# Mixture-of-experts kernel: down products two chunks behind gate and up, chains cut one group apart, tokens scaled once by 1/rms, and the gather's modulation on ACT

## The chip, the cores and the metric

One Trainium2 chip, one of its cores. The metric is the device time of one execution in microseconds, as a median over runs. The profiled execution is one more run, with its own time and its own span.

## The reference, cut to what matters

The model has two layers on 256 latent tokens of width 1024. Layer 0 is attention, a short convolution and a dense SwiGLU; layer 1 is a spatial gating unit and then eight SwiGLU experts, of which every token uses the best two. All of it is fp32. The change concerns the experts, for which the tokens are first normalised by their rms and modulated (a scale and a shift for each feature):

```python
def modulate(x, g, shift, scale):
    return rmsnorm(x, g) * (1 + scale) + shift

def moe_swiglu(h, router_w, wg, wu, wd):
    logits = (h @ router_w).astype(jnp.float32)
    top_v, top_i = lax.top_k(logits, TOP_K)              # 2 of 8
    gates = jax.nn.softmax(top_v, axis=-1)
    dense_gate = ...                                      # 0 where not chosen
    out = jnp.zeros_like(h)
    for e in range(N_EXPERTS):                            # 8, each 3584 wide
        out = out + dense_gate[..., e:e + 1] * swiglu(h, wg[e], wu[e], wd[e])
    return out
...
    hf = modulate(h, norm_ffn_g[i], sf, cf)
    h = h + gf * moe_swiglu(hf, router_w[j], moe_w_gate[j], moe_w_up[j], moe_w_down[j])
```

## The kernel before

**Experts, chunks, groups, tiles.** The expert stage streams all weights of all eight experts through the core. An expert's 3584 hidden features are cut into seven chunks of 512. A chunk takes six weight tiles of 1 MB (128 partitions by 2048 fp32): two for gate, two for up, two for down. Two tiles are one *group*, and the program is a list of groups, made in the same order in `Weights.__init__` (for the loads) and in the loop at the end (for the work): gate of chunk ci, up of chunk ci, down of chunk ci−1. So the down product of an expert's last chunk comes behind gate and up of the next expert's chunk 0.

**Splits.** TensorE works on fp32 values that are split into a high and a low part. For each tile `Weights.split` issues an ACT cast of the raw tile `mw` to its high part `mh` and a DVE subtraction that gives the low part `ml`. There are six raw buffers, five for high parts and five for low parts. SP issues the next load when the split of an old tile has released its buffer. `group` issues the splits of the tiles a few ahead, and behind the second of three it runs what is in the list `late`.

**Light and heavy experts.** The tokens of an expert are gathered by a one-hot matrix product into at most 128 rows. With at most 64 tokens ("light") the token operand holds high and low part side by side, and each k-slice takes two matmuls of 512 columns (`products`, lines 1078 and 1079); otherwise ("heavy") it takes three (`mm3`, lines 142 to 144). Which of the two a group runs is decided on TensorE by a branch on a count in memory.

**The chain of a chunk.** TensorE makes the gate and up rows (`m_0_0`, `m_0_1`), ACT copies them to SBUF (line 1138), TensorE turns them (line 1146), ACT makes the silu of gate (`m_sg`, line 1152), DVE multiplies with up (line 1153), ACT and DVE split the result into high and low part, `moe_aT` (lines 217 and 218), and the down product reads that (`m_y`). `moe_aT` has two buffers.

**The chain of an expert.** *Gather*, in the preceding expert: DVE makes six one-hot tiles (lines 1098 and 1101), of which `ohs` carries the factor 1/rms of each token; TensorE multiplies `h` by it (line 1109); the result is modulated by `m_m.a` and `m_m.b` out of PSUM, four instructions on DVE for the first half of the features (line 1118) and four on ACT for the second (line 1116), and split to `m_xg`. *Scatter*, in the following expert: behind the last down product DVE scales `m_y` (line 1173, `m_yg`), ACT and DVE split it (`m_yhi`, `m_ylo`), and four scatter products `m_sc` (line 1182) are each added to `moe_acc` by a DVE instruction (line 1184). For expert 0 that instruction reads `h` in place of `moe_acc`.

**What sets the order.** Every engine executes in program order, and that order is decided when the program is built: by the lists `late` and `todo_after` of the loop, and by a scheduler behind them. A DVE instruction that waits for TensorE holds every split that stands behind it.

Of the kernel before, what the change touches and what calls it, by code (L numbers as in the profile page):

```python
# [18 lines left out]
P = 128  # L19
D = 1024  # L20
KT = D // P
S = 256
# [52 lines left out]
def hybrid_kernel(  # L75
# [185 lines left out]

    def ada_rows(pa, name, w=512):
        rw = xp.tile([P, 512], F32, tag="rw", name=name + "_rw", bufs=2)
        A.copy(rw[:, :w], pa[:, :w])
        flush()
        return rw
# [59 lines left out]
    def ada_v(layer, n, half):  # L326

        r = ada_load(layer, n, half)
        if half == 0:
            held[0] = xp.tile([P, 512], F32, tag="rw", name=f"adv{layer}_{n}", bufs=2)  # L330
# [576 lines left out]

    class Weights:
# [86 lines left out]
    h = slot(2, "h")[:, :NT * D].rearrange("p (t d) -> p t d", t=NT)  # L995
    for t in range(NT):
        for b in range(2):
# [3 lines left out]
            copied = A.copy(h[:, t, b * 512:(b + 1) * 512], pt)  # L1001
# [45 lines left out]
    acc = slot(4, "moe_acc")[:, :NT * D].rearrange("p (t d) -> p t d", t=NT)  # L1047
# [38 lines left out]
    class Expert:  # L1086


        def __init__(self, e, pos, xg_slot, n):
            self.e, self.n, self.pos = e, n, pos  # L1090
            self.xg = in_pairs(slot(xg_slot, n + "_xg", F32R)[:, :2 * KT * P], KT)

        def positions(self):
            oh2 = x2k(self.n + "_oh")
            self.oh, self.ohs = oh2[:, :S], oh2[:, S:]
            self.ohd = x2k(self.n + "_ohd")[:, :S]
            for t in range(NT):
                V.tensor_scalar(self.ohs[:, t * P:(t + 1) * P], iota, one(self.pos, t, self.e), rstd[t], op0=ALU.is_equal, op1=ALU.mult)
# [4 lines left out]
        def gather(self, b, pool=None):  # L1103
            n = self.n
            pg = bank(f"{n}_pg{b}", pool or psd)
            for i in range(4):
                k = 4 * b + i
                for t in range(NT):
                    T.matmul(pg[:, i * P:(i + 1) * P], h[:, t, k * P:(k + 1) * P], self.ohs[:, t * P:(t + 1) * P],
                             start=(t == 0), stop=(t == NT - 1))  # L1110
# [39 lines left out]
        def act(self, ci, pts):  # L1150
# [3 lines left out]
            self.aT = in_pairs(at[:, 1024 * (ci % 2):1024 * (ci % 2) + 1024], 4)  # L1154
            split_pairs(self.aT, sg)

        def down(self, ci, parts, light):
            aT = self.aT
# [7 lines left out]
        def down_half(self, i, parts, light):  # L1166

            for k in range(4):
                products(self.y[i], self.aT, k, tuple(w[:, k, :] for w in parts[0]), light, False, k == 3)

        def gated(self, i):
            src = x2k(f"{self.n}_yg{i}")
            V.tensor_tensor(src, self.y[i], gf1[:, i * 512:(i + 1) * 512], op=ALU.mult)
            y = [x2k(f"{self.n}_y{x}{i}", F32R) for x in ("hi", "lo")]
# [3 lines left out]
        def scatter(self, t, i, y, first=False, pool=None):  # L1178
# [4 lines left out]
            av, was = (a[:, t, i * 512:(i + 1) * 512] for a in (acc, h if first else acc))  # L1183
            V.scalar_tensor_tensor(av, ps, one(gate, t, self.e), was, op0=ALU.mult, op1=ALU.add)
# [16 lines left out]
    for b in range(2):  # L1201
        ex.gather(b, psb)
    behind["V"] = ex.made.ins
    W.load(8)
    lights = [None] * NE
    step, todo_after = 0, {}

    def after(n, f):
        todo_after.setdefault(step + n, []).append(f)

    late = []

    def group(light, body, then=lambda: None):
# [11 lines left out]
        late.append(then)  # L1225
# [161 lines left out]
```

## Time and profile before

| | |
|---|---|
| median of 3 runs (lowest to highest) | 1474.3 us (1472.17 to 1477.77) |
| profiled execution: device time, span | 1478.5 us, 1476.7 us |
| PE busy in the span | 1390.9 us (94%) |
| DVE busy | 1226.8 us (83%) |
| ACT busy | 974.0 us (66%) |
| the expert stage, from the first `m_ohT` to the end | 968.8 us |

PE is TensorE, PEld its weight loads, DVE is VectorE, ACT is ScalarE. An expert's begin is taken here as the moment at which ACT writes its `m_ohT`: 507.87, 629.92, 745.22, 861.17, 977.15, 1106.34, 1237.31 and 1352.98 us. The experts 0, 4 and 5 run heavy, the other five light. A busy share is an average over stages with different limits; the rows further down are taken from single stages.

### The profile page before, as it was taken

Reading aid. Unit: us, or ns where it says so; the run is one execution under the profiler, and the core shown is the slowest. Engines: PE = TensorE matmul, PEld = TensorE weight load, DVE = VectorE, ACT = ScalarE, POOL = GpSimd, SP = SyncE. Lnnn points to the kernel's source line nnn. Section 1 sums busy time; section 2 is a strip of 40 time slices with the busy share of each in tenths; the row PEclk is TensorE's granted clock in tenths of the full one; section 3 lists DMA queues with packets and bytes.
Section 4 is the critical chain, followed back from the end, with each engine's and each line's share of the span. In section 5 each row is a group of like instructions: output and inputs, shape, how many; then the busy total and the mean of one; then the engine's idle time right before and its main releaser. Section 6 shows DMA issues by size and latency. Waiting matters only on the chain.

```text
span 1476.7 us, 19854 instructions
## 1 busy us (share of the span) xinstructions
PE 1390.9 (94%) x7746; PEld 1151.7 (78%) x7746; DVE 1226.8 (83%) x1256; ACT 974.0 (66%) x891; POOL 1.9 (0%) x7
## 2 busy tenths in 40 slices
PE   6999999999999999999989989999999999899897
PEld 4667789999979888877767767777888888677675
DVE  4687588776666698899999998998888879899897
ACT  3444354433354576788887887886777768788785
POOL 0000000000000000000000000000000000000000
PEclk9999999999999999999999999999999999999999
DMA  9554488776654698899998998998978988899894
GB/s 367 226 219 166 155 335 323 286 274 251 245 224 176 240 402 330 326 340 395 403 398 343 408 398 334 416 385 338 365 294 331 365 343 349 331 421 386 336 413 189
DMA packets 66784, 473.53 MB, mean 321 GB/s; under 512 B 7376, under 2 KB 7760, under 8 KB 9696
## 3 DMA queue, kind: packets, MB, share of 16 engines
q1 hardware_dynamic: 66464, 471.16, 82.0%
q8 instruction: 93, 1.52, 0.4%
q0 software_dynamic: 192, 0.56, 0.2%
q14 instruction: 35, 0.29, 0.1%
HBM read 470.64 MB, written 1.05 MB: 319 GB/s over the span
## 4 chain that ended last, share of the span: by engine, by line
PE 59%; DVE 20%; issue 9%; ACT 8%; DMA 5%; DVEq 0%; SPq 0%; ACTq 0%
DVE ml L949 13%; ACT mh L948 5%; PE m L142 5%; PE m L144 5%; PE m L143 5%; PE fg_ps L164 4%; PE fd L164 4%; PE fu_ps L164 4%; PE m_y L144 2%; PE m_y L142 2%; PE m_y L143 2%; PE so_ps L164 2%; PE ada L259 2%; PE su_ps L164 2%; DMA mw<-in_moe_w_gate_dram 1%
## 5 line engine op out<-in xcount | busy, mean ns | idle before, releaser
L949 DVE TENSOR_TENSOR ml<-mw,mh 128x2048 fp32r<-128x2048 f32 x336 | 757.1, 2286 | 47.9 <-ACT mh L948 44.9
L948 ACT CAST mh<-mw 128x2048 fp32r<-128x2048 f32 x336 | 631.2, 1910 | 12.4 <-PE so_ps L164 4.1
L1079 PE MATMUL m<-ml,m_xg 128*128 128x512 f32 x560 | 223.3, 399 | 5.7 <-DVE ml L949 5.7
L1078 PE MATMUL m<-mh,m_xg 128*128 128x512 f32 x560 | 224.1, 400 | 0.0
L1078 PE MATMUL m_y<-mh,moe_aT 128*128 128x512 f32 x280 | 118.2, 422 | 25.3 <-DVE moe_aT L218 21.4
L142 PE MATMUL m<-mh,m_xg 128*128 128x512 f32 x336 | 134.5, 401 | 0.6 <-ACT m_xg L217 0.6
L1079 PE MATMUL m_y<-ml,moe_aT 128*128 128x512 f32 x280 | 121.3, 433 | 13.8 <-DVE ml L949 11.9
L1079 PEld LDWEIGHTS m<-ml,m_xg 128*128 128x128 f32 x560 | 105.2, 188 | 37.0 <-DVE ml L949 14.6
L144 PE MATMUL m<-mh,m_xg 128*128 128x512 f32 x336 | 132.9, 396 | 0.0
L143 PE MATMUL m<-ml,m_xg 128*128 128x512 f32 x336 | 132.7, 395 | 0.0
L1078 PEld LDWEIGHTS m<-mh,m_xg 128*128 128x128 f32 x560 | 105.3, 188 | 22.6
L1079 PEld LDWEIGHTS m_y<-ml,moe_aT 128*128 128x128 f32 x280 | 56.4, 201 | 45.3 <-DVE ml L949 34.3
L1078 PEld LDWEIGHTS m_y<-mh,moe_aT 128*128 128x128 f32 x280 | 56.7, 203 | 41.3 <-ACT mh L948 19.3
L217 ACT CAST moe_aT<-m_sg 128x512 fp32r<-128x512 f32 x56 | 37.4, 669 | 72.5 <-DVE m_sg L1153 72.5
L142 PEld LDWEIGHTS m<-mh,m_xg 128*128 128x128 f32 x336 | 65.6, 195 | 13.3 <-ACT m_xg L217 1.5
L144 PEld LDWEIGHTS m<-mh,m_xg 128*128 128x128 f32 x336 | 65.5, 195 | 12.5
L143 PEld LDWEIGHTS m<-ml,m_xg 128*128 128x128 f32 x336 | 65.7, 196 | 11.9
L1152 ACT ACTIVATE m_sg<-m_t 128x512 f32<-128x512 f32 x56 | 33.6, 599 | 53.5 <-PE m L142 26.7
L144 PE MATMUL m_y<-mh,moe_aT 128*128 128x512 f32 x168 | 66.4, 396 | 0.7 <-DVE moe_aT L218 0.7
L143 PE MATMUL m_y<-ml,moe_aT 128*128 128x512 f32 x168 | 66.4, 395 | 0.0
L142 PE MATMUL m_y<-mh,moe_aT 128*128 128x512 f32 x168 | 66.2, 396 | 0.0
L164 PE MATMUL fd<-a,fd_hi 128*128 128x256 f32 x352 | 63.0, 281 | 0.0
(410 smaller groups left out, 2663.8 us busy)
## 6 DMA issues: line engine op xcount, KB each, us to landing
mw<-in_moe_w_gate_dram SPq DMA_DIRECT2D x112, 1024.0 KB, 7.1
mw<-in_moe_w_up_dram SPq DMA_DIRECT2D x112, 1024.0 KB, 7.1
mw<-in_moe_w_down_dram SPq DMA_DIRECT2D x110, 1024.0 KB, 6.8
ada<-in_ada_w_dram SPq DMA_DIRECT2D x40, 1024.0 KB, 4.9
fg_w<-in_ffn_w_gate_dram SPq DMA_DIRECT2D x11, 1024.0 KB, 5.2
fu_w<-in_ffn_w_up_dram SPq DMA_DIRECT2D x11, 1024.0 KB, 5.4
fd<-in_ffn_w_down_dram SPq DMA_DIRECT2D x11, 1024.0 KB, 5.0
adap<-in_ada_pairs_dram SPq DMA_DIRECT2D x8, 1024.0 KB, 9.6
```

Of the source, the lines that this page charges most:

```text
L142: T.matmul(o, lh, rh, start=start, stop=False)
L143: T.matmul(o, lh, rl, start=False, stop=False)
L144: T.matmul(o, ll, rh, start=False, stop=stop)
L164: self.newest = m = T.matmul(o, lhsT, rhs, start=self.first is None, stop=stop, skip_group_check=True)
L217: A.copy(hi, src)
L259: queued(T.matmul(pa[32 * j:32 * j + 32, :r.shape[2]], stat[:, 4 * half + j, :], r[:, j, :], start=(first and half == 0), stop=(last and h ...
L948: queued(A.copy(hi, r), "A")
L949: queued(V.tensor_tensor(lo, r, hi.bitcast(F32), op=ALU.subtract), "V")
L1078: T.matmul(o, x, wh, start=start, stop=False)
L1079: T.matmul(o, x, wl, start=False, stop=stop)
L1152: A.activation(sg, pts[0], AF.Silu)
```

## The change

It does five things.

1. The down product of a chunk stands two chunks behind its gate and up (`LAG`), in the order of loads and of work; `moe_aT` gets a third buffer. At the program's end one whole down group, that of chunk 5, stands ahead of the two half groups of chunk 6.
2. One list `todo` takes the place of `late` and `todo_after`: the split of `moe_aT`, of `m_yg` and of a gathered half is put a group behind the instructions that make its input.
3. `h` is written as token times 1/rms, out of PSUM by ACT, and a second ACT copy of the same PSUM tile starts `moe_acc` with the unscaled token. So the one-hot tiles need no factor (`ohs` and its two DVE instructions for each expert are gone), and the first addition of a scatter reads `moe_acc` like the others.
4. All eight modulations of a gather are on ACT.
5. The two row buffers `rw` of an earlier stage become halves of one tile, and the third `moe_aT` buffer takes that place later.

```diff
+    LAG = 2
...
-                    if ci:
-                        self.add(self.down(e, ci - 1))
-                    elif e:
-                        self.add(self.down(e - 1, NCH - 1))
+                    if e or ci >= LAG:
+                        self.add(self.down(*divmod(e * NCH + ci - LAG, NCH)))
+            for ci in range(NCH - LAG, NCH - 1):
+                self.add(self.down(NE - 1, ci))
...
-            copied = A.copy(h[:, t, b * 512:(b + 1) * 512], pt)
+            at_ = slice(b * 512, (b + 1) * 512)
+            A.copy(acc[:, t, at_], pt)
+            copied = A.activation(h[:, t, at_], pt, AF.Copy, scale=rstd[t])
...
-            for t in range(NT):
-                V.tensor_scalar(self.ohs[:, t * P:(t + 1) * P], iota, one(self.pos, t, self.e), rstd[t], op0=ALU.is_equal, op1=ALU.mult)
...
-                if b:
-                    A.activation(t32[:, o], pg[:, o], AF.Identity, bias=m_m.b(k), scale=m_m.a[:, k:k + 1])
-                else:
-                    V.tensor_scalar(t32[:, o], pg[:, o], m_m.a[:, k:k + 1], m_m.b(k), op0=ALU.mult, op1=ALU.add)
-            self.made = split_pairs(self.xg[:, 4 * b:4 * b + 4], t32)
+                A.activation(t32[:, o], pg[:, o], AF.Identity, bias=m_m.b(k), scale=m_m.a[:, k:k + 1])
+            self.part[b] = t32
+
+        def cut(self, b):
+            self.made = split_pairs(self.xg[:, 4 * b:4 * b + 4], self.part.pop(b))
...
-            self.aT = in_pairs(at[:, 1024 * (ci % 2):1024 * (ci % 2) + 1024], 4)
-            split_pairs(self.aT, sg)
+
+            def cut():
+                self.aT[ci] = in_pairs(at[((self.e * NCH if isinstance(self.e, int) else 0) + ci) % 3], 4)
+                split_pairs(self.aT[ci], sg)
+
+            return cut
...
-            if n == tiles.stop + 2:
-                while late:
-                    late.pop(0)()
+                for f in todo.pop(step, ()):
+                    f()
...
+    def put_back(x):
+
+        def gate_out():
+            src = [x.gated(i) for i in range(2)]
+
+            def cut():
+                ys = [x.gated_parts(i, src[i]) for i in range(2)]
+                for i in range(2):
+                    for t in range(NT):
+                        then(1 + 2 * i + t, lambda t=t, i=i: x.scatter(t, i, ys[i]))
+
+            then(1, cut)
+
+        then(0, gate_out)
+
+    def gathered(x, b):
+        x.gather(b)
+        then(1, lambda: x.cut(b))
...
+    for ci in range(NCH - LAG, NCH - 1):
+        group(lights[-1], lambda parts, arm: ex.down(ci, parts, arm))
```

The order is shown at three places. The first is DVE where expert 2 takes over from expert 1; `m1_` and `m2_` are the two experts, `ml92` is the low part of weight tile 92, `m2_0_sg` belongs to chunk 0 of expert 2. Before:

```order
L1184 SCALAR_TENSOR_TENSOR moe_acc_4885<-m1_sc00_7633,gate_4792,moe_acc_4885 128x512
L949 TENSOR_TENSOR ml92_7500<-mw92_7318,mh92_7499 128x2048
L1153 TENSOR_TENSOR m2_0_sg_7569<-m2_0_t1_7479,m2_0_sg_7569 128x512
L949 TENSOR_TENSOR ml93_7564<-mw93_7370,mh93_7563 128x2048
L218 TENSOR_TENSOR moe_aT_4884<-m2_0_sg_7569,moe_aT_4884 128x512
L1184 SCALAR_TENSOR_TENSOR moe_acc_4885<-m1_sc10_7693,gate_4792,moe_acc_4885 128x512
...
L949 TENSOR_TENSOR ml94_7577<-mw94_7380,mh94_7576 128x2048
L1184 SCALAR_TENSOR_TENSOR moe_acc_4885<-m1_sc01_7774,gate_4792,moe_acc_4885 128x512
L949 TENSOR_TENSOR ml95_7626<-mw95_7427,mh95_7625 128x2048
```

In the changed kernel the same engine has there:

```order
L1163 TENSOR_TENSOR m2_0_sg_7484<-m2_0_t1_7406,m2_0_sg_7484 128x512
L957 TENSOR_TENSOR ml89_7409<-mw89_7234,mh89_7408 128x2048
L218 TENSOR_TENSOR moe_aT3_4874<-m2_0_sg_7484,moe_aT3_4874 128x512
...
L1201 SCALAR_TENSOR_TENSOR moe_acc_4827<-m1_sc00_7744,gate_4777,moe_acc_4827 128x512
L957 TENSOR_TENSOR ml96_7607<-mw96_7418,mh96_7606 128x2048
L1163 TENSOR_TENSOR m2_1_sg_7684<-m2_1_t1_7594,m2_1_sg_7684 128x512
L957 TENSOR_TENSOR ml97_7671<-mw97_7482,mh97_7670 128x2048
L218 TENSOR_TENSOR moe_aT_4873<-m2_1_sg_7684,moe_aT_4873 128x512
...
L1201 SCALAR_TENSOR_TENSOR moe_acc_4827<-m1_sc10_7808,gate_4777,moe_acc_4827 128x512
L957 TENSOR_TENSOR ml98_7690<-mw98_7493,mh98_7689 128x2048
L1201 SCALAR_TENSOR_TENSOR moe_acc_4827<-m1_sc01_7882,gate_4777,moe_acc_4827 128x512
```

The low part of chunk 0's `moe_aT` has moved from behind tile 93 to behind tile 89, and what stands beside the scatter is now the chain of chunk 1. Between tile 89 and the first addition stand tiles 90 to 95, the two `m_yg` and the two `m_ylo`.

The second place is TensorE at the same point, around the down product of expert 2's chunk 0 (the light branch). Before:

```order
L1182 MATMUL m1_sc10_7693<-m1_yhi0_7489,m1_ohT_5985 128x512
L1182 MATMUL m1_sc10_7693<-m1_ylo0_7490,m1_ohT_5985 128x512
...
L1078 MATMUL m2_y0_7623<-mh92_7499,moe_aT_4884 128x512
...
L1079 MATMUL m2_y1_7624<-ml93_7564,moe_aT_4884 128x512
...
L1182 MATMUL m1_sc01_7774<-m1_yhi1_7495,m1_ohT_5985 128x512
L1182 MATMUL m1_sc01_7774<-m1_ylo1_7496,m1_ohT_5985 128x512
```

Now:

```order
L1199 MATMUL m1_sc10_7808<-m1_yhi0_7676,m1_ohT_5932 128x512
L1199 MATMUL m1_sc10_7808<-m1_ylo0_7677,m1_ohT_5932 128x512
...
L1089 MATMUL m2_y0_7736<-mh96_7606,moe_aT3_4874 128x512
...
L1090 MATMUL m2_y1_7737<-ml97_7671,moe_aT3_4874 128x512
...
L1199 MATMUL m1_sc01_7882<-m1_yhi1_7680,m1_ohT_5932 128x512
L1199 MATMUL m1_sc01_7882<-m1_ylo1_7681,m1_ohT_5932 128x512
```

TensorE's own order at the scatter is the same as before: second scatter, down product of the new expert's chunk 0, third scatter. What moved is the pair of tiles that this down product reads, from 92 and 93 to 96 and 97, against `moe_aT` that is ready earlier.

The third place is ACT where the expert stage begins (`mo` is the PSUM tile with the tokens, `mo_v` is 1/rms, `mh2` and `mh3` are weight splits, `m0_` is expert 0). Before:

```order
L1001 COPY h_4842<-mo01_4849 128x512
L1001 COPY h_4842<-mo10_4855 128x512
L1031 ACT_TABLE_LOAD
L1031 ACTIVATE ex0_5127<-lg_4867,mx0_5124 128x8
...
L1001 COPY h_4842<-mo11_4861 128x512
L948 CAST mh2_4946<-mw2_4932 128x2048
L948 CAST mh3_4952<-mw3_4934 128x2048
...
L217 CAST m0_xg_4891<-m0_t0_4909 128x512
```

Now:

```order
L1011 ACTIVATE h_4826<-mo00_4828,mo_v_4808 128x512
L1011 ACTIVATE h_4826<-mo01_4835,mo_v_4808 128x512
...
L1010 COPY moe_acc_4827<-mo10_4842 128x512
L1011 ACTIVATE h_4826<-mo10_4842,mo_v_4808 128x512
L1010 COPY moe_acc_4827<-mo11_4849 128x512
L1011 ACTIVATE h_4826<-mo11_4849,mo_v_4808 128x512
L956 CAST mh2_4932<-mw2_4918 128x2048
L956 CAST mh3_4938<-mw3_4920 128x2048
L1125 ACTIVATE m0_t0_4895<-m0_pg0_4886,modT_103,a_m_4050 128x128
...
L217 CAST m0_xg_4880<-m0_t0_4895 128x512
```

Ahead of the casts of tiles 2 and 3 there are now eight PSUM reads in place of four, two of them behind a wait for 1/rms; behind the casts stand the first half's four modulations, which were on DVE, ahead of the first `m0_xg`.

## Rows read from the trace of the kernel before

**Rows 1.** The profile's page: busy time of the engines, and the costliest group.

```profile
PE 1390.9 (94%) x7746; PEld 1151.7 (78%) x7746; DVE 1226.8 (83%) x1256; ACT 974.0 (66%) x891; POOL 1.9 (0%) x7
...
L949 DVE TENSOR_TENSOR ml<-mw,mh 128x2048 fp32r<-128x2048 f32 x336 | 757.1, 2286 | 47.9 <-ACT mh L948 44.9
```

**Rows 2.** Windows by expert (0, 1, 2, 7): length, busy times, TensorE clock, DMA share, GB/s.

```profile
507.87:629.92 122.05, 121.80 (x571) 102.87 (x571) 104.14 (x70) 90.20 (x75) 0.00 (x0) 1.00 0.91 348
629.92:745.22 115.30, 106.25 (x514) 83.88 (x513) 111.20 (x78) 97.55 (x82) 0.00 (x0) 1.00 0.97 380
745.22:861.17 115.95, 104.46 (x492) 81.50 (x491) 110.17 (x77) 95.04 (x80) 0.00 (x0) 0.97 0.96 382
1352.98:1476.70 123.72, 103.59 (x466) 78.96 (x464) 109.69 (x72) 90.23 (x74) 0.00 (x0) 0.95 0.81 324
```

**Rows 3.** DVE's waits, experts 2 and 3 (745.22 to 977.15 us): us in total, times, longest.

```profile
DVE moe_acc L1184 <- PE m_sc L1182: 8.9, 2, 4.5
DVE ml L949 <- ACT mh L948: 2.7, 4, 1.2
```

**Rows 4.** The same for the light experts 6 and 7 (1237.31 to 1460 us).

```profile
DVE moe_acc L1184 <- PE m_sc L1182: 8.5, 2, 4.3
```

**Rows 5.** Timeline of DVE as expert 2 takes over: start, duration, [idle before <-releaser].

```profile
768.80 0.69 DVE L218 TENSOR_TENSOR moe_aT<-m_sg,moe_aT 128x512 fp32r<-128x512 f32 x1
...
776.78 0.75 DVE L1184 SCALAR_TENSOR_TENSOR moe_acc<-m_sc,gate,moe_acc 128x512 f32<-128x512 f32 x1 [4.43 <-PE m_sc L1182]
```

**Rows 6.** Timeline of TensorE at the same place.

```profile
769.64 0.76 PE L1078 MATMUL m_y<-mh,moe_aT 128*128 128x512 f32 x1 [4.59 <-DVE moe_aT L218]
...
776.12 0.40 PE L1182 MATMUL m_sc<-m_yhi,m_ohT 128*128 128x512 f32 x1
776.35 0.39 PE L1182 MATMUL m_sc<-m_ylo,m_ohT 128*128 128x512 f32 x1
```

**Rows 7.** Windows, columns as in Rows 2: behind that wait, and a stretch of light chunks.

```profile
772.00:776.00 4.00, 4.00 (x12) 3.13 (x11) 0.35 (x1) 3.05 (x2) 0.00 (x0) 0.56 0.96 358
1400.00:1450.00 50.00, 47.76 (x231) 37.50 (x230) 50.00 (x29) 44.34 (x36) 0.00 (x0) 1.00 1.01 410
```

**Rows 8.** Timeline of DVE: one one-hot tile with its factor, and a gather's modulations.

```profile
703.52 0.34 DVE L1098 TENSOR_SCALAR m_oh<-cst,posm,mo_v 128x128 f32<-128x128 f32 x1
...
717.02 0.40 DVE L1118 TENSOR_SCALAR m_t<-m_pg,a_m,modT 128x128 f32<-128x128 f32 x1
...
719.55 1.04 DVE L1118 TENSOR_SCALAR m_t<-m_pg,a_m,modT 128x128 f32<-128x128 f32 x3
```

**Rows 9.** Timeline of ACT: the other half's modulations.

```profile
723.40 1.50 ACT L1116 ACTIVATE m_t<-m_pg,modT,a_m 128x128 f32<-128x128 f32 x4 [0.33 <-PE m_pg L1109]
```

**Rows 10.** Timeline of ACT where the expert stage begins.

```profile
494.49 1.07 ACT L1001 COPY h<-mo 128x512 f32<-128x512 f32 x2 [0.16 <-PE mo L1000]
...
499.87 0.58 ACT L1001 COPY h<-mo 128x512 f32<-128x512 f32 x1
500.35 3.70 ACT L948 CAST mh<-mw 128x2048 fp32r<-128x2048 f32 x2
```

**Rows 11.** Timeline of TensorE at the same place: the first gather and the first expert matmul.

```profile
501.20 3.73 PE L1109 MATMUL m_pg<-m_oh,h 128*128 128x128 f32 x32
...
506.65 0.51 PE L142 MATMUL m<-mh,m_xg 128*128 128x512 f32 x1 [0.64 <-ACT m_xg L217]
```

**Rows 12.** Timeline of DVE at the end of the program.

```profile
1455.92 4.49 DVE L949 TENSOR_TENSOR ml<-mw,mh 128x2048 fp32r<-128x2048 f32 x2
1460.33 0.69 DVE L1153 TENSOR_TENSOR m_sg<-m_t,m_sg 128x512 f32<-128x512 f32 x1
1461.72 0.69 DVE L218 TENSOR_TENSOR moe_aT<-m_sg,moe_aT 128x512 fp32r<-128x512 f32 x1 [0.71 <-ACT moe_aT L217]
1464.70 0.69 DVE L1173 TENSOR_TENSOR m_yg<-m_y,gf 128x512 f32<-128x512 f32 x1 [2.28 <-PE m_y L1079]
```

**Rows 13.** The page's DMA issues: KB each, us to landing.

```profile
mw<-in_moe_w_gate_dram SPq DMA_DIRECT2D x112, 1024.0 KB, 7.1
```

More of the change, by code (lines that the diff above doesn't have):

```diff
@@ L329, in ada_v @@
         if half == 0:
-            held[0] = xp.tile([P, 512], F32, tag="rw", name=f"adv{layer}_{n}", bufs=2)
+            held[0] = next_rows()
         ac = held[0]
@@ L994, in hybrid_kernel @@
     rstd = st.rstd()
-    h = slot(2, "h")[:, :NT * D].rearrange("p (t d) -> p t d", t=NT)
+    h, acc = (slot(i, n)[:, :NT * D].rearrange("p (t d) -> p t d", t=NT) for i, n in ((2, "h"), (4, "moe_acc")))
     for t in range(NT):
@@ L1046, in hybrid_kernel @@
     at = slot(3, "moe_aT", F32R)
-    acc = slot(4, "moe_acc")[:, :NT * D].rearrange("p (t d) -> p t d", t=NT)
+    at3 = xp.tile([P, 1024], F32R, tag="rw", name="moe_aT3", bufs=1)
+    at = [at[:, :1024], at[:, 1024:2048], at3]
     iota = cst[:, C_IOTA:C_IOTA + P]
@@ L1176, in gated, with scatter @@
             return y
-        def scatter(self, t, i, y, first=False, pool=None):
+        def scatter(self, t, i, y, pool=None):
             ps = bank(f"{self.n}_sc{t}{i}", pool or psd)
@@ L1182, in scatter @@
                 T.matmul(ps, self.ohT[:, t * P:(t + 1) * P], y[o], start=(o == 0), stop=(o == 1))
[L1183 to L1184 removed]
+            av = acc[:, t, i * 512:(i + 1) * 512]
+            V.scalar_tensor_tensor(av, ps, one(gate, t, self.e), av, op0=ALU.mult, op1=ALU.add)
     def store(t, i):
@@ L1202, in hybrid_kernel @@
         ex.gather(b, psb)
+        ex.cut(b)
     behind["V"] = ex.made.ins
@@ L1205, in hybrid_kernel, with then, group @@
     lights = [None] * NE
[L1206 to L1213, printed above, removed]
+    step, todo = 0, {}
+    def then(n, f):
+        todo.setdefault(step + n, []).append(f)
+    def group(light, body):
         nonlocal step
@@ L1230, in turned, with acted @@
         pts = [bank(f"{x.n}_{ci}_t{m}", psb) for m in range(2)]
-        return pts, (lambda arm: x.turn(pts, gu, arm)), (lambda: x.act(ci, pts))
-    nothing = (None, lambda arm: None, lambda: None)
-    prev = None
+        def acted():
+            cut = x.act(ci, pts)
+            then(1, cut)
+        return (lambda arm: x.turn(pts, gu, arm)), acted
+    def put_back(x):
[6 more added lines that the diff above has]
+                        then(1 + 2 * i + t, lambda t=t, i=i: x.scatter(t, i, ys[i]))
+            then(1, cut)
+        then(0, gate_out)
+    def gathered(x, b):
+        x.gather(b)
+        then(1, lambda: x.cut(b))
+    experts = {0: ex}
     for e in range(NE):
-        light = lights[e]
+        light, ex = lights[e], experts[e]
         for ci in range(NCH):
+            turn = None
+            if ci:
+                turn, acted = turned(ex, ci - 1, gu)
+                behind.clear()
             gu = []
-            _, turn, acted = turned(ex, ci - 1, prev[2]) if ci else nothing
-            if ci:
-                behind.clear()
             o = bank(f"{ex.n}_{ci}_0")
@@ L1264, in hybrid_kernel @@
                 flush()
-            if prev is not None:
-                px, pi, _ = prev
+            if e or ci >= LAG:
+                pe, pi = divmod(e * NCH + ci - LAG, NCH)
+                px, turn = experts[pe], None
                 if pi == 0:
@@ L1269, in hybrid_kernel @@
                 if ci == NCH - 1:
[L1270 to L1272 removed]
+                    turn, acted = turned(ex, ci, gu)
                 def downs(parts, arm):
                     px.down(pi, parts, arm)
[L1276 to L1286 removed]
+                    if turn:
+                        turn(arm)
+                group(lights[pe], downs)
+                if turn:
+                    then(0, acted)
+                if pi == NCH - 1:
+                    put_back(px)
             if ci == NCH - 3 and e + 1 < NE:
[L1288 removed]
+                nxt = experts[e + 1] = Expert(e + 1, posm, (e + 1) % 2, f"m{e + 1}")
                 nxt.positions()
                 for b in range(2):
[L1291 to L1293 removed]
+                    then(1 + b, lambda b=b, x=nxt: gathered(x, b))
         if e + 1 < NE:
[L1295 removed]
             lights[e + 1] = nc.values_load(few[0:1, e + 1:e + 2], engines=(mybir.EngineType.PE,), min_val=0, max_val=1)
+    for ci in range(NCH - LAG, NCH - 1):
+        group(lights[-1], lambda parts, arm: ex.down(ci, parts, arm))
     for i in range(2):
[L1298 to L1299 removed]
+        group(lights[-1], lambda parts, arm: ex.down_half(i, parts, arm))
+        y = ex.gated_parts(i, ex.gated(i))
         for t in range(NT):
[L1301 removed]
+            ex.scatter(t, i, y, pool=psb)
             store(t, i)
@@ L1312, in hybrid_kernel @@
                 ex.gather(b)
+                ex.cut(b)
             ex.po = bank("v_ohp", psb)
```

68 lines of the change are left out of this document (27 added, 41 removed).

## The prediction

> **What bounds the kernel now.** I began with the page: TensorE is busy 94% of the span, DVE 83%, and DVE's largest item by far is 336 splits `ml` of 2.29 us [rows 1]. Such averages mix stages, so next I cut the expert stage at each expert's begin. A heavy expert, 0, has TensorE busy 121.80 of 122.05 us: TensorE is the bound, and DVE's waits there cost nothing. A light expert, 2, takes 115.95 us with TensorE busy 104.46 and DVE 110.17: DVE is nearest to the bound, and the 5.8 us in which it does nothing are the thing to explain [rows 2]. The view of waits explains them: in experts 2 and 3 together DVE lost 8.9 us in two waits of `moe_acc` for a scatter product, one at each begin, and 2.7 us in four waits for ACT's cast; in experts 6 and 7 it lost 8.5 us in two waits [rows 3, 4]. The timeline of one such wait shows how it arises. DVE finishes the low part of chunk 0's `moe_aT` at 769.5 (768.80 + 0.69), and TensorE, idle for 4.59 us, starts that chunk's down product only then, at 769.64. It executes in order, so the third scatter product stands behind the whole down product, and DVE's addition for it stands ahead of the next splits. The 16 matmuls of the product take 6.48 us (769.64 to 776.12), 0.40 each, where the two behind them start 0.23 apart (776.12, 776.35), and the window behind the idle time has a granted clock of 0.56, about the lower of the clock's two levels, 1.2 GHz. The addition comes at 776.78 after 4.43 us of idle [rows 5 to 7]. So 17.4 us (8.9 + 8.5) of the span are one stall, four times. Expert 1 lacks it.
>
> **The change part by part.**
>
> *Down two chunks behind.* At that place the down product of chunk 0 now uses tiles 96 and 97, and `moe_aT` is cut behind tile 89. DVE has seven splits of 2.2 us between the two, 15 us, so the product has its input long before its weights. The third scatter then waits only for TensorE's own work. Behind split 97 DVE still does a `moe_aT`, an addition and split 98, 0.7 + 0.7 + 2.2 = 3.6 us, ahead of the addition that waited; TensorE needs for the eight matmuls on tile 97 and two scatters some 2.3 us at the full clock. That leaves about a microsecond of margin, and I take the whole 17.4 us as gained; the bounds are 17.4 and, if TensorE comes that far late again, 0. What may be late next is the first scatter on TensorE: the two `m_yg` stand together now and `m_ylo` comes 0.7 us later behind its split. DVE's first addition stands a split later as well, so it isn't held.
>
> *DVE's work.* For each later gather DVE loses two one-hot instructions and four modulations: 2 × 0.34 + 0.40 + 1.04 = 2.1 us of durations, 1.8 us of engine time, since an instruction begins some 0.08 us before the last one ends (two splits last 4.49 us, and the next begins 4.41 behind the first's start) [rows 8, 12]. The gathers for experts 2, 3, 4 and 7 lie in light experts (1, 2, 3 and 6): 4 × 1.8 = 7.2 us. Those in experts 4 and 5 lie under TensorE's bound and give nothing.
>
> *ACT's work.* ACT takes four modulations more for each gather, 1.5 us [rows 9], and is busy 95 of 116 us in expert 2 [rows 2]; it has 15 us to spare even if the expert shrinks to 110. But they stand in front of a cast for which DVE may wait. Today these waits cost a light expert 2.7 / 2 = 1.35 us [rows 3]. From below nothing is added; from above the whole 1.5 us and its echo at a second cast, 3 us an expert. I take 0.8 us an expert, nearer to nothing because the average slack is large: 5 × 0.8 = 4 us lost.
>
> *Begin of the expert stage.* ACT must read each PSUM tile twice: four more instructions of 0.53 us (1.07 for two), and the first two scaled copies wait for 1/rms. Behind them stand the two casts of 3.70 us, and behind these the four modulations that DVE did before, 1.5 us [rows 9, 10]. Before, the gather began at 501.20 and the first expert matmul came at 506.65, behind the cast of `m_xg` [rows 11]. Now the last token copy ends some 1.5 to 2 us later, near 502; with casts of 3.7, modulations of 1.5 and 0.5, and the `m_xg` cast of 0.6 the first matmul is near 509. Its second half waits for another weight cast. Expert 0 is bound by TensorE, so the delay goes through: 3 us lost, between 1 and 5.
>
> *The end.* Before, the last split ended at 1460.4, and then came the product with up, the split of `moe_aT`, and half the last down product, until `m_yg` began at 1464.70 [rows 12]. Now the chain of chunk 6 has a whole down group as cover, and behind the last split stand only the second half's eight matmuls. DVE's `m_sg` and low part move ahead of the last split and delay it by 1.2 us. The second `m_yg` came eight matmuls of 0.23 later, near 1466.6; now it comes at 1460.4 + 1.2 + 2.3 = 1463.9. Gain 2.7, say 2.8 us; between 1 and 4.
>
> *The rest.* In the middle of an expert the splits of `moe_aT` stood a tile apart from their inputs already, and their order hardly moves: 0. Four one-hot tiles share one buffer, `rw` becomes one tile: 0, they lie in stages whose order is the same row by row. Heavy experts: 0.
>
> **The sum.** −17.4 − 7.2 + 4 + 3 − 2.8 = −20.4 us. The profiled execution took 1478.5 us (span 1476.7), so it would become 1458.1. The median of the runs is 4.2 us lower, 1474.3, which gives 1453.9; I say 1454.
>
> **The transfers.** A light expert would shrink to 115.95 − 4.45 − 1.8 + 0.8 = 110.5 us. It moves 42 tiles of 1.049 MB, 44.04 MB, so DMA must bring 399 GB/s, against 382 now [rows 2]. A stretch of 50 us without stalls shows 410 at a DMA share of 1.01 [rows 7]; at that rate an expert takes 107.4 us. And a load lands 7.1 us after its issue [rows 13]: at 400 GB/s that is 2.8 MB on the way, under three of the six raw buffers, so the others hold tiles that wait for DVE. I conclude that DMA comes close and doesn't bind.
>
> The Trainium skill speaks against the change here: its page "HBM Reference", section Specifications (TRN2), puts the effective bandwidth at about 358 GB/s for a core when both cores of a pair stream, and at about 425 for one that streams alone. By the first a light expert would be an estimated 123 us and no work taken from DVE could help; by the second it would be an estimated 103.6 us. The trace sides with the second: 382 GB/s over a whole expert, 410 over 50 us.
>
> **The rivals.**
>
> *A. DMA binds.* For it: its share is 0.96 in light experts and 1.01 where it moves 410 [rows 2, 7], so it has no idle time to give. Against it: the landing time above, and that a stall of DVE lets buffers fill. If light experts can't go below 113 us (390 GB/s), experts 2, 3 and 6 gain 2.9 each, expert 7 some 4, expert 1 about 1.8: 14.5 us in place of 20.6 (17.4 + 7.2 − 4). Sum −14.3: 1460. At 382 GB/s there is nothing to gain: 1474.
>
> *B. No new waits, and the old ones for the cast shrink.* Then the 4 us are not lost, and another 3 to 5 are gained: 1446. For it: ACT's average slack. Against it: DVE catches up with ACT as its stalls vanish.
>
> *C. The stall moves.* At an expert's begin TensorE still has to pass down product and scatters in order. If the first scatter, whose `m_ylo` comes later now, idles TensorE long enough that the clock falls as it did at 772 us [rows 7], the third scatter is late again and 2 to 4.4 us of each of the four stalls stay: −20.4 + 8 to 17.4, 1462 to 1471. If the order of splits allows no gain at all, 1474.
>
> *D. Slower: ACT becomes the bound of light experts.* The modulations read PSUM and wait for the gather on TensorE, and ACT in order holds every cast behind them, on DVE's critical path. It would need a wait of some 0.8 us for each of the 35 light chunks to eat the 20.4 us, and 1.1 us to pass the threshold below: then 1482. Against it: ACT's idle share of 18% and waits of 1.35 us a whole expert today [rows 2, 3].
>
> **How the numbers follow.** I give the forecast 0.55 (1448 to 1459), A 0.17, B 0.10, C 0.13 and D 0.05. A change of under 0.5%, 7.4 us, can't be told from none with this kernel; the threshold for faster is 1466.9. The forecast, B, most of A (0.13) and half of C (0.06) lie below: 0.84 faster. The rest of A and C, 0.11, is within; D is slower. The range reaches from B's upper gain, 1441, to where A and C begin to lose the effect, 1466.
>
> **What would show it.** Right: DVE's waits of `moe_acc` for `m_sc` fall from 8.9 and 8.5 us to under 2 in the same experts; no window with a clock near 0.56 behind an expert's begin; light experts of 109 to 112 us at 395 to 404 GB/s; DVE's busy time in one down by 1.8 us; the first expert matmul 2 to 4 us later against the stage before; `m_yg` of the last half some 3.5 us behind the last split. A is right if light experts end with DVE waiting for ACT's cast while ACT waits for `mw`. C is right if TensorE idles ahead of `m_sc` and `moe_acc` still waits. D is right if DVE's waits for `mh` exceed 5 us in a light expert. The forecast is wrong above all if the four stalls are not on the path, because the transfers they hold back are what sets the pace.

## The result and the profile after

The changed kernel takes 1451.12 us (median of 4 runs, 1449.14 to 1453.82), the kernel before 1473.8 in the same set: a ratio of 0.9844, 95% interval 0.983 to 0.9859, 22.7 us less. A later set gave 0.9837 (0.9817 to 0.9856). The forecast was 1454. The profiled execution has a span of 1452.0 us, 24.7 less than the one of before.

To see where the 22.7 us went I cut both traces at DVE's split of every 42nd tile, which is an expert's worth of weights. The last column is the prediction's sum, spread over the same stretches.

| stretch, from split to split | before, us | changed, us | difference | forecast |
|---|---|---|---|---|
| ahead of split 0 | 479.97 | 478.07 | −1.9 | 0 |
| 0 to 42: stage begins, expert 0 (heavy) | 147.46 | 152.64 | +5.2 | +3 |
| 42 to 84: expert 1 (light) | 114.32 | 112.82 | −1.5 | −1.0 |
| 84 to 126: expert 2 (light) | 115.94 | 110.04 | −5.9 | −5.4 |
| 126 to 168: expert 3 (light) | 115.98 | 110.02 | −6.0 | −5.5 |
| 168 to 210: expert 4 (heavy) | 129.20 | 125.64 | −3.6 | 0 |
| 210 to 252: expert 5 (heavy) | 130.97 | 130.85 | −0.1 | 0 |
| 252 to 294: expert 6 (light) | 115.67 | 110.57 | −5.1 | −5.2 |
| 294 to 335: expert 7 (light) | 108.62 | 104.09 | −4.5 | −3.5 |
| split 335 to the end | 18.62 | 17.31 | −1.3 | −2.8 |

The first line is not the change's: its split 0 stands between 475.0 and 479.97 us in the traces of this study, whatever the kernel. Without it the trace shows 22.8 us, what the medians show. A second trace of the changed kernel repeats all light experts to within 0.06 us, but it has 151.43 us in the second line and 18.55 in the last, differences of +4.0 and −0.1: the two ends vary by a microsecond from run to run.

The page of the changed kernel: busy times of the engines, and among the costliest groups the down product of light experts with its wait for `moe_aT`, which was 21.4 us before.

```profile
PE 1382.3 (95%) x7746; PEld 1149.5 (79%) x7746; DVE 1213.6 (84%) x1208; ACT 986.2 (68%) x927; POOL 1.9 (0%) x7
...
L1089 PE MATMUL m_y<-mh,moe_aT 128*128 128x512 f32 x280 | 111.7, 399 | 3.3 <-DVE moe_aT L218 3.3
```

DVE lost 13.2 us of work [rows 1], and TensorE waits for `moe_aT` once in the whole program.

Windows of the changed kernel in the columns of [rows 2], for experts 2 and 3, again from `m_ohT` to `m_ohT`:

```profile
741.33:851.35 110.02, 102.11 (x492) 81.45 (x491) 108.52 (x71) 96.23 (x84) 0.00 (x0) 0.98 1.00 403
851.35:961.37 110.02, 101.08 (x492) 79.77 (x491) 108.54 (x71) 96.11 (x85) 0.00 (x0) 1.00 1.00 402
```

DVE is busy 108.5 of 110.0 us. Its waits in these two experts, where [rows 3] had two lines, are one line:

```profile
DVE ml L957 <- ACT mh L956: 3.0, 8, 0.7
```

The timeline of DVE and then of TensorE as expert 2 takes over, the place of [rows 5, 6]:

```profile
757.44 0.68 DVE L218 TENSOR_TENSOR moe_aT<-m_sg,moe_aT 128x512 fp32r<-128x512 f32 x1
...
782.78 0.74 DVE L1201 SCALAR_TENSOR_TENSOR moe_acc<-m_sc,gate,moe_acc 128x512 f32<-128x512 f32 x1
```

```profile
775.50 0.40 PE L1089 MATMUL m_y<-mh,moe_aT 128*128 128x512 f32 x1
776.65 0.50 PE L1090 MATMUL m_y<-ml,moe_aT 128*128 128x512 f32 x1 [0.75 <-DVE ml L957]
...
781.42 0.40 PE L1199 MATMUL m_sc<-m_ylo,m_ohT 128*128 128x512 f32 x1
```

`moe_aT` is ready 17 us ahead of the product that reads it. The product is paced by its weights (0.75 us behind `ml`), the two scatter matmuls end at 781.8, and the addition at 782.78 has no wait: the margin is 1 us, as worked out.

One sign that the prediction named is missing all the same. Behind expert 2's begin the granted clock does fall, about to the lower of its two levels, after TensorE has waited 1.75 us for a DVE addition ahead of the next scatter product:

```profile
784.00:788.00 4.00, 4.00 (x20) 3.83 (x19) 4.00 (x3) 3.36 (x3) 0.00 (x0) 0.57 0.96 363
```

It cost nothing that shows: expert 2 took 110.04 us with this fall, expert 3, whose clock is 1.00 throughout, 110.02.

At the program's end, DVE and TensorE:

```profile
1434.73 2.28 DVE L957 TENSOR_TENSOR ml<-mw,mh 128x2048 fp32r<-128x2048 f32 x1
1436.93 0.68 DVE L218 TENSOR_TENSOR moe_aT<-m_sg,moe_aT 128x512 fp32r<-128x512 f32 x1
1439.91 0.69 DVE L1187 TENSOR_TENSOR m_yg<-m_y,gf 128x512 f32<-128x512 f32 x1 [2.29 <-PE m_y L1090]
```

```profile
1437.76 0.48 PE L1089 MATMUL m_y<-mh,moe_aT 128*128 128x512 f32 x1 [3.25 <-DVE moe_aT L218]
```

Here the split of `moe_aT` stands behind the last weight split as before [rows 12], and TensorE waits 3.25 us for it. Behind this wait the clock stays at 1.00. In the second trace TensorE waits 3.32 us at the same place, the clock of the product behind it is 0.63 (1438.5 to 1441.5 us), and the end is 1.2 us longer.

### The profile page after: what moved, and what is told of

Its sections match the earlier page's. It is cut to its first block, busy times and chain, and to the rows that moved or that the text cites. A ratio compares the mean times of both kernels' runs of the same rounds, so it can differ in the third digit from the quotient of the medians.

```text
span 1452.0 us, 19805 instructions
## 1 busy us (share of the span) xinstructions
PE 1382.3 (95%) x7746; PEld 1149.5 (79%) x7746; DVE 1213.6 (84%) x1208; ACT 986.2 (68%) x927; POOL 1.9 (0%) x7
## 4 chain that ended last, share of the span: by engine, by line
PE 62%; DVE 18%; issue 8%; ACT 8%; DMA 4%; SPq 0%; DVEq 0%; ACTq 0%
DVE ml L957 12%; PE m L144 5%; PE m L142 5%; PE m L143 5%; ACT mh L956 5%; PE fg_ps L164 4%; PE fd L164 4%; PE fu_ps L164 4%; PE m_y L142 3%; PE m_y L144 3%; PE m_y L143 3%; PE ada L259 2%; PE so_ps L164 2%; PE su_ps L164 2%; PE m L1090 1%
## 5 line engine op out<-in xcount | busy, mean ns | idle before, releaser
L1090 PE MATMUL m_y<-ml,moe_aT 128*128 128x512 f32 x280 | 116.3, 415 | 18.9 <-DVE ml L957 17.6
L1089 PE MATMUL m_y<-mh,moe_aT 128*128 128x512 f32 x280 | 111.7, 399 | 3.3 <-DVE moe_aT L218 3.3
L1090 PEld LDWEIGHTS m_y<-ml,moe_aT 128*128 128x128 f32 x280 | 53.1, 190 | 49.6 <-DVE ml L957 39.0
L143 PE MATMUL m_y<-ml,moe_aT 128*128 128x512 f32 x168 | 66.3, 395 | 0.0
L144 PE MATMUL m_y<-mh,moe_aT 128*128 128x512 f32 x168 | 66.3, 395 | 0.0
L142 PE MATMUL m_y<-mh,moe_aT 128*128 128x512 f32 x168 | 65.8, 395 | 0.0
L1089 PEld LDWEIGHTS m_y<-mh,moe_aT 128*128 128x128 f32 x280 | 53.2, 190 | 14.3 <-issue 3.7
```

The source lines that it names most:

```text
L142: T.matmul(o, lh, rh, start=start, stop=False)
L143: T.matmul(o, lh, rl, start=False, stop=False)
L144: T.matmul(o, ll, rh, start=False, stop=stop)
L1089: T.matmul(o, x, wh, start=start, stop=False)
L1090: T.matmul(o, x, wl, start=False, stop=stop)
```

## The experiments

My theory after the result: the light experts are bound by DVE, the distance of two chunks took the four stalls, and the rest is DVE's lighter gather less what ACT's extra work costs. The rivals: transfers at 400 GB/s set the 110 us; or the gain comes from the moved modulations or the steps, not the distance. Ratios are to the kernel before, run on the same chip in the same set.

| kernel | ratio | 95% interval | median, us |
|---|---|---|---|
| changed, again | 0.9837 | 0.9817 to 0.9856 | 1451.83 |
| lag1 | 0.9964 | 0.9952 to 0.9976 | 1470.57 |
| cut_now | 0.9836 | 0.9815 to 0.9857 | 1453.25 |
| mod_dve | 0.9977 | 0.9963 to 0.9991 | 1472.47 |
| mod_late | 0.9822 | 0.9805 to 0.9839 | 1450.75 |
| mod8_late | 0.9873 | 0.9847 to 0.9898 | 1456.79 |
| act_twice | 0.991 | 0.9886 to 0.9935 | 1461.72 |
| cheap_lo | 1.0164 | 1.0142 to 1.0186 | 1500.02 |
| more_bytes | 1.0012 | 0.9995 to 1.0029 | 1477.72 |
| bytes_pinned | 1.0179 | 1.015 to 1.0208 | 1499.64 |
| ends | 0.982 | 0.9796 to 0.9843 | 1448.46 |
| best | 0.9823 | 0.9801 to 0.9844 | 1449.2 |

**lag1.** The distance is undone, and with it the extra group ahead of the split of `moe_aT`, which cut_now tests without the distance.

```diff
-    LAG = 2
+    LAG = 1
...
-            cut = x.act(ci, pts)
-            then(1, cut)
+            x.act(ci, pts)()
```

Expected: 

> The changed kernel with the down product one chunk behind again (and moe_aT cut without the extra group, which one chunk of distance does not allow); all else as changed. If the four stalls at the begin of experts 2, 3, 6 and 7 came from that distance and were worth their whole length, they come back: DVE waits of moe_acc for m_sc of about 4.4 us each, a clock near 0.56 behind them, and 16 to 18 us more than the changed kernel, about 1468. If most of the gain came from DVE's lighter gather and the stalls were partly hidden by transfers that caught up, the time stays within 8 us of the changed kernel, under 1460.

Measured: 1470.57 us, 0.012 of the kernel before (17 to 19 us) more than the changed kernel. DVE's waits in its experts 2 and 3, and TensorE's at the begin of expert 2:

```profile
DVE moe_acc L1201 <- PE m_sc L1199: 6.5, 2, 3.3
```

```profile
771.46 0.47 PE L1089 MATMUL m_y<-mh,moe_aT 128*128 128x512 f32 x1 [4.46 <-DVE moe_aT L218]
```

The wait for `moe_aT` is that of [rows 6] again, and the granted clock in the window behind it (772 to 776 us) is 0.57. DVE's two waits are shorter than the 4.4 us that I expected; with 7.8 us in two waits in experts 6 and 7, 14.3 of the 17.4 us are back. The four light experts concerned are 3.4, 3.3, 4.8 and 3.5 us longer than in the changed kernel. So the distance gives about 18 of the 22.7 us. All else together gives the 0.0036 (5 us) by which lag1 beats the kernel before; no run takes the one-hot tiles by themselves.

**cut_now.** The steps a group apart are undone: the three splits are called where their inputs are made.

```diff
-            cut = x.act(ci, pts)
-            then(1, cut)
+            x.act(ci, pts)()
...
-        then(1, lambda: x.cut(b))
+        x.cut(b)
```

(and the same for `gated_parts` in `put_back`.)

Expected: 

> The changed kernel without the steps a group apart: moe_aT, the scaled y and the gathered half are cut right behind the instructions that make them. TensorE's order is the same row for row; ACT's and DVE's differ in some 40 rows, pairs that change places. If the steps matter little, as the prediction has it, within 2 us of the changed kernel. If they are what took the waits away, the waits of moe_acc or of the casts return and it is 5 us or more slower.

Measured: 0.9836, light experts of 110.12 us. The steps do nothing that these runs can tell from none, as the prediction had it.

**mod_dve, mod_late, mod8_late.** The modulations of the later gathers go back to DVE. In mod_dve it is the first half's four:

```diff
-                A.activation(t32[:, o], pg[:, o], AF.Identity, bias=m_m.b(k), scale=m_m.a[:, k:k + 1])
+                if b or not isinstance(self.e, int) or self.e == 0:
+                    A.activation(t32[:, o], pg[:, o], AF.Identity, bias=m_m.b(k), scale=m_m.a[:, k:k + 1])
+                else:
+                    V.tensor_scalar(t32[:, o], pg[:, o], m_m.a[:, k:k + 1], m_m.b(k), op0=ALU.mult, op1=ALU.add)
```

Expected: 

> The changed kernel with the first half's four modulations of a gather back on DVE, for all experts but the first. If DVE sets the pace of light experts, experts 1, 2, 3 and 6 each become 1.3 us longer, 5 us in all, about 1456. If DMA or ACT set it, the time stays within 1.5 us of the changed kernel, or falls by up to 3 us because ACT has less in front of its casts.

Measured: 1472.47, 20 us more than the changed kernel and four times what I expected; light experts of 113.7 us. The timelines of ACT and DVE in expert 2 show waits that neither kernel had at this length (ACT's wait for the gather is 0.33 us in [rows 9] and 1.2 in expert 2 of the changed kernel):

```profile
831.58 1.16 ACT L1126 ACTIVATE m_t<-m_pg,modT,a_m 128x128 f32<-128x128 f32 x3 [3.48 <-PE m_pg L1119]
832.63 1.90 ACT L956 CAST mh<-mw 128x2048 fp32r<-128x2048 f32 x1
```

```profile
834.56 2.29 DVE L957 TENSOR_TENSOR ml<-mw,mh 128x2048 fp32r<-128x2048 f32 x1 [3.82 <-ACT mh L956]
```

The edit made the scheduler put the last two of the 16 matmuls of the second half's gather behind a whole group of gate and up. ACT, in order, waits for them ahead of a cast, and DVE for the cast. If that is the cause, moving ACT's four modulations behind more casts must cure it. In mod_late they are issued with the cut (the rest of the edit, which moves them into a function of their own, is left out):

```diff
+            if b and isinstance(self.e, int) and self.e:
+                self.modulated(b)
             self.made = split_pairs(self.xg[:, 4 * b:4 * b + 4], self.part.pop(b)[0])
```

Expected: 

> As mod_dve, four modulations of a gather on DVE, but the four that stay on ACT are issued a group later, with the cut. TensorE's order and DVE's work are those of mod_dve; in ACT's queue two more casts now stand ahead of the modulations. If mod_dve lost its 21 us because ACT, waiting for the last two gather matmuls, held a cast, that wait goes and only DVE's 1.3 us an expert stay: 1455 to 1460. If it lost them through the modulations on DVE themselves, it stays near 1472.

Measured: 0.9822, 1450.75 us. The whole loss is gone, with TensorE's order and DVE's work of mod_dve: the place of the modulations cost the 20 us, not their engine. More than that, with four of the eight on DVE the light expert is as long as with none, 110.07 against 110.04. DVE is busy 1.1 us longer in it (109.64 against 108.53) and waits less for casts, 0.8 us in experts 2 and 3 together in place of 3.0:

```profile
DVE ml L957 <- ACT mh L956: 0.8, 4, 0.2
```

mod8_late puts all eight on DVE, at the places of mod_late.

Expected: 

> As mod_late, but all eight modulations of the later gathers on DVE, none on ACT: DVE gets 1.3 us an expert more than in mod_late, where it was busy 219.3 of 220.1 us in experts 2 and 3. If DVE's work sets the pace of light experts, each of 1, 2, 3 and 6 becomes 0.9 to 1.3 us longer than 110.07, some 4 us in all. If the 110 us are set by the transfers at 400 GB/s, they stay, and DVE is simply busy in what was waiting.

Measured: 1456.79; the light experts 1, 2, 3 and 6 are 0.9 us longer each than in mod_late (110.97 in expert 2). Its window there:

```profile
742.15:853.12 110.97, 101.21 (x492) 79.62 (x491) 110.74 (x80) 93.53 (x76) 0.00 (x0) 1.00 1.00 400
```

DVE has next to no idle time left to give, and its work shows in the length: here DVE sets the pace. (The whole run is 6 us longer than mod_late; the four experts account for 3.6 of them, and in the traces expert 7 and the end for 2.0.)

**act_twice.** Every modulation of the later gathers is issued twice on ACT.

```diff
-                A.activation(t32[:, o], pg[:, o], AF.Identity, bias=m_m.b(k), scale=m_m.a[:, k:k + 1])
+                for _ in range(1 if not isinstance(self.e, int) or self.e == 0 else 2):
+                    A.activation(t32[:, o], pg[:, o], AF.Identity, bias=m_m.b(k), scale=m_m.a[:, k:k + 1])
```

Expected: 

> The changed kernel with every modulation of the later gathers issued twice on ACT, 3 us more of ACT work an expert and none elsewhere. If ACT has the slack that its busy time of 96 in 110 us suggests, DVE's waits for the cast grow by under 1 us an expert: within 5 us of the changed kernel, about 1454. If work in front of the casts lands on the path at full size, 3 us for each of experts 1, 2, 3 and 6 and something in the heavy ones: 1463 or more.

Measured: 1461.72; the four light experts 2.5 us longer each (112.48 in expert 2). DVE's waits in experts 2 and 3 together:

```profile
DVE ml L957 <- ACT mh L956: 7.3, 12, 1.0
```

So 3 us more of ACT work (2.8 more of busy time) lengthen a light expert by 2.5, though ACT is busy 96 of 110 us in the changed kernel. Its slack is not where the casts are: in the same experts of the changed kernel ACT waits for DVE's `m_sg` some 12 us an expert, and that is most of its idle time. I read it so: behind each such wait ACT is little ahead of DVE, and what stands in front of a cast then reaches DVE.

**cheap_lo.** A third of the low parts becomes an instruction with one operand (and loses its value).

```diff
+                if n % 3 == 2:
+                    queued(V.tensor_scalar(lo, r, 0.0, None, op0=ALU.mult), "V")
+                else:
+                    queued(V.tensor_tensor(lo, r, hi.bitcast(F32), op=ALU.subtract), "V")
```

Expected: 

> The changed kernel with every third low part replaced by a product with zero of the raw tile, one operand instead of two (the low part of 112 of the 336 tiles is left out of the sums). Transfers, casts and matmuls stay. If DVE alone sets the pace of light experts, each loses up to 14 times the difference of the two instructions, up to 14 us with half the duration, until the next limit; DMA at 420 GB/s is 105 us. If DMA already binds at 403 GB/s, light experts stay within 1 us of 110 and DVE idles behind ACT's casts, which wait for mw. I expect 105 to 107.5 us for an expert, 12 to 22 us in all, with waits for mw.

Measured: 1500.02, slower than the kernel before. Both expectations fell. DVE has 109 us less work, and expert 2 takes 118.8 us in which no engine is full: TensorE is busy 104.4 us, DVE 95.3, ACT 96.4, and DMA moves 375 GB/s.

In experts 2 and 3 DVE waits 29.4 us for casts, 8.4 for the high part of `moe_aT` and 7.8 for the scatter. The new order differs in many rows, and I did not separate which of them makes the waits. The run says nothing on the transfers.

**more_bytes and bytes_pinned.** 64 KB more is loaded for each tile from the 42nd on, into a tile that nobody reads.

```diff
+                if n >= 42:
+                    src = self.tiles[n][0]
+                    more = nc.sync.dma_start(extra[n % 2], (src[0] if isinstance(src, list) else src.rearrange("p (k f) -> p k f", k=2))[:, 0, :EX])
...
+    EX = 128
+    extra = [kp.tile([P, EX], F32, name=f"extra{i}") for i in range(2)]
```

Expected: 

> The changed kernel with 64 KB more loaded ahead of every weight tile from the 42nd on, into a tile that nothing reads: at least 6% more transfer, nothing else. At 110 us a light expert would then need 425 GB/s. If DMA already sets the pace at 403, light experts become 117 us and the whole about 30 us longer, 1480. If it has the margin up to the 420 or so of its fastest stretches, 111 to 113 us an expert, 4 to 12 us in all, about 1459. If it is far from binding, no change.

Measured: 1477.72, but not by the experiment as meant: the scheduler sent the first loads ahead, some by hundreds of us, and only from 911 us on did they stand beside their tiles. Expert 2, without them, took 110.05 as in the changed kernel. Expert 6, with them, took 112.95 (110.57 in the changed kernel) and expert 7 took 112.6 (104.09). In bytes_pinned each one is tied into the queue right ahead of its tile (edit not shown). The 406 to 414 GB/s that I read from this run are the tiles' bytes over the two experts' times; windows over these experts show 404 and 390.

Expected: 

> As more_bytes, but each 64 KB load is pinned in SP's queue right ahead of its weight tile; in more_bytes the first 130 of them ran early and only experts from the fourth on had them beside their tiles. A light expert then brings 46.8 MB. If DMA can do 406 to 414 GB/s, as experts 6 and 7 of more_bytes showed, light experts take 113 to 115 us, in all 12 to 25 us more than the changed kernel, with ACT's casts waiting for mw. If DMA were no limit near 400, they stay at 110.

Measured: 1499.64. The window of expert 2, the largest of ACT's waits for tiles in experts 2 and 3, and the largest of SP's waits in expert 2:

```profile
743.83:861.86 118.03, 103.86 (x491) 80.53 (x490) 109.49 (x71) 98.61 (x84) 0.00 (x0) 0.99 1.01 399
```

```profile
ACT mh L965 <- DMA mw<-in_moe_w_up_dram: 10.0, 16, 1.0
```

```profile
SPq L947 <- DMA extra<-in_moe_w_down_dram: 27.6, 14, 2.9
```

With 6% more bytes casts wait 24.6 us for tiles in the two experts, so loads do hold them. But the edit brought a second limit. There are two `extra` buffers, so an extra load is issued only when the one two tiles earlier has landed, and SP, which issues in order, holds the weight loads behind it. SP waits 79.7 of 118 us in expert 2 for such landings. Whether the bytes, their rows of 512 bytes or the two buffers took the 8 us stays open, and the run doesn't show where DMA's limit lies. The same bytes cost expert 6 only 2.4 us.

In the changed kernel SP's waits in expert 2 are for DVE, and over 40 us DMA moved more than the 399 GB/s above:

```profile
SPq L116 <- DVE ml L957: 90.8, 41, 3.1
```

```profile
740.00:780.00 40.00, 36.70 (x167) 28.02 (x166) 40.00 (x28) 34.26 (x29) 0.00 (x0) 1.00 1.01 422
```

The casts wait 0.2 us for tiles in experts 2 and 3 together, so the tiles are there before they are wanted, and SP waits 90.8 of 110 us until DVE has freed a buffer. So there the loads follow DVE, and transfers do not set the 110 us.

**ends and best.** ends changes what the prediction's two ends had lost or missed: the second token tile's copies to `moe_acc` and expert 0's first four modulations are on DVE, and the last chunk's `moe_aT` is cut ahead of the last split.

```diff
-            A.copy(acc[:, t, at_], pt)
+            (V.tensor_copy if t else A.copy)(acc[:, t, at_], pt)
...
-            then(1, cut)
+            if (x.e, ci) == (NE - 1, NCH - 1):
+                behind["V"] = cut().ins
+            else:
+                then(1, cut)
```

(Left out are expert 0's modulations, and that the last three groups run the list `todo` ahead of their splits.)

Expected: 

> The changed kernel with three moves at the two ends of the expert stage: the second token tile's copy to moe_acc on DVE, the first half's modulations of expert 0 on DVE, and the last chunk's moe_aT cut ahead of the last split. If the late first matmul of expert 0 passes through to the end (its TensorE has no idle time), the first two give 1.5 to 2.5 us; the last gives 1 to 2 us, since TensorE then waits for the last split and not for moe_aT. In all 3 to 4 us less than the changed kernel, about 1447.5. If either end is covered by something else, under 1.5 us.

Measured: 0.982, 1448.46 us. The first expert matmul comes 27.8 us behind split 0 (29.6 and 28.4 in the two traces of the changed kernel, 26.7 before), but expert 1 is 1.0 us longer (113.80 us). The end comes 14.5 us behind the last split (17.3 and 18.5), and expert 7, ahead of it, is 0.8 us longer:

```profile
1430.61 0.69 DVE L218 TENSOR_TENSOR moe_aT<-m_sg,moe_aT 128x512 fp32r<-128x512 f32 x1 [0.71 <-ACT moe_aT L217]
1431.22 2.29 DVE L957 TENSOR_TENSOR ml<-mw,mh 128x2048 fp32r<-128x2048 f32 x1
```

best adds mod_late to it.

Expected: 

> The moves of ends and of mod_late together: the begin of the expert stage and the last chunk as in ends, and for the later gathers four modulations on DVE with ACT's four issued a group later. If the gains at the two ends add to a stage in which the light experts stay at 110 us, 3 to 4 us less than the changed kernel, about 1448. If mod_late's order takes back what the ends give, no less than 1451.

Measured: 0.9823, 1449.2 us, 2.6 less than the changed kernel in the same set. The intervals of best, ends and the changed kernel overlap; the traces show the program's end 14.5 us long in both, shorter than in any other, and mod_late adds nothing to that.

## Why the prediction was right, point by point

**The four stalls.** Right in mechanism and size. 17.4 us were put down to them; they are gone from the trace, experts 2, 3, 6 and 7 lost 21.5 us in all, and lag1 brings 15.0 us of that back in these four. What was to be late next, the first scatter, is: TensorE waits 0.8 us for `m_ylo` in expert 2, and in experts 2 and 3 DVE waits for nothing but casts. Rival C is out: the clock still falls behind expert 2's begin, but no stall comes of it.

**DVE's and ACT's work.** The signs were right, the sizes were not. Against [rows 2, 3], DVE's busy time in experts 2 and 3 is 1.6 us less each (1.8 forecast) and its waits for casts are 0.15 us longer (0.8 forecast), so an expert gained 1.5 us beside its stall where 1.0 was forecast. Expert 1, which had no stall, shows the 1.5 by itself. In expert 6 DVE's idle time beside the stall grew by 0.7 us (1.3 to 2.0), in expert 7 by 0.4, in expert 1 not at all. So ACT's price was some 1.4 us over the five, not 4. The prediction had also charged it to five experts, though expert 7 holds no gather. Rival B was half right: the 4 us were hardly lost, but the old waits for the cast did not shrink.

Why the price was so low is not shown. mod_late doesn't tell, since it also issues ACT's own four modulations later: it has 1.1 us more of DVE work than the changed kernel and 1.1 us less of waits for casts, and so the same length. act_twice shows that more work on ACT does land on the path, at 2.5 us for 3. That is above the price taken, 0.8 for 1.5, and under the upper bound, 3 for 1.5. The reason given for 0.8 us, ACT's large average slack, was the weak step: the slack lies in waits for DVE. My reading is that before, with four modulations on ACT, part of the price was paid already.

**The begin.** 3 us were forecast, between 1 and 5. Measured from split 0 the first expert matmul is 1.8 to 2.9 us later. The table's second line has 2.3 us more than that in both traces, and expert 4 gained 3.6 us that nobody forecast. These are partly one effect of the cut at every 42nd tile: with the new distance other work lies in a stretch. The profile has 12 TensorE matmuls more in the first stretch (787 against 775) and 12 fewer in expert 4's (582 against 594), where a light down group stands in place of a heavy one. That is argued from the order and these counts; the stretches of heavy experts and the begin together gave +1.5 us, in the second trace +0.3, where +3 was forecast.

**The end.** Wrong in its step, not in its sign. It said that DVE's `m_sg` and low part move ahead of the last split; `m_sg` did, the low part did not (1436.93 behind 1434.73), TensorE still waited, and 1.3 us came in place of 2.8, in the second trace 0.1. ends moved it, and its end is 4.1 us shorter than before.

**The sum.** That it came within 3 us is partly luck: the light experts gave 2.4 us more than forecast (23.0 against 20.6), the begin with the heavy experts cost 1.5 us less, and the end gave 1.5 us less. Two smaller sums of the prediction don't come out. Rival B's upper gain, by its own terms, ends at 1445 and not at the 1441 with which the range begins. And rival D's 0.8 us in each of 35 chunks is 28 us, which already gives its 1482; 0.6 us would eat the 20.4.

**The transfers.** 399 GB/s were said to be needed and to be had; the trace has 403. Rival A's sign, ACT waiting for `mw`, is absent, and SP waits for DVE. How far off the limit is no run shows. Of the two figures in the Trainium skill, "HBM Reference", section Specifications (TRN2), the trace bears out the one for a core alone as the nearer: 403 GB/s over 110 us and 422 over 40, against its 425.

**D, slower.** It did not happen, but mod_dve shows that it was close by: one wait of ACT for the gather ahead of a cast in each expert, the mechanism of rival D, cost 20 us there, nearly all of the gain.

## What to carry to other kernels

An in-order engine should not stall on a chain that one more chunk of distance would hide; here the gain was about the whole stall, and it could be read beforehand from one timeline. An engine's average idle time is no cover for work put in front of what another engine waits for: look at what it waits for itself. Whether transfers set the pace is read from how long their readers wait for tiles, not from the share of time in which DMA is busy. And after any edit under a scheduler, read where the moved instructions landed; the same work at another place cost 20 us or nothing.

## What the runs showed of the hardware

- The one-operand product of 128x2048 fp32 took 1.22 us on DVE, the subtraction with two operands 2.29.
- TensorE's idle time of 3.9 to 4.6 us at the four begins of before was each time followed by matmuls 0.43 us apart, at a granted clock of 0.50 in windows of 2 us; a wait of 4.46 us in lag1 by a window of 0.57. A wait of 1.75 us in expert 2 of the changed kernel was followed by 0.57, the same wait in expert 3 was not; and of its two waits of 3.3 us at the program's end, in two traces, one was followed by 0.63 and one by 1.00.
- DMA moved 402 to 403 GB/s over a light expert of the changed kernel at a share of 1.00, 422 over 40 us of it at 1.01, and 365 over 20 us (785 to 805) at 0.97: a share near 1 did not mean that no more could be moved.
